# A two-layer decoder step on one Trainium2 core: RMS norms by sums with tokens on partitions, own buffers for raw mixer weights, other orders at the start of gate/up and in the down rounds, wider feature rows

## The chip, the cores and the metric

The kernel runs on one core of a Trainium2 chip. Its engines are TensorE (PE in the profile, with weight loads as PEld), VectorE (DVE), ScalarE (ACT), GpSimd (POOL) and SyncE (SP), which issues most DMAs; POOL issues others. The metric is the device time of one execution in microseconds (us). Before the change it is 2952.68 us, the median of 3 runs (2951.64 to 2955.0).

## The reference

One inference step of a two-layer decoder: an mLSTM layer (layer 0), then a forgetting-attention layer (layer 1). There are 1104 token rows (16 meta tokens, 1024 prompt, 64 sample rows), D_MODEL is 1024, D_FF 2816. Each layer ends with the output projection of its mixer, added to the residual stream, and a SwiGLU block; between the layers a value/key projection of layer 1 reads the normed stream. Only the following is touched by the change:

```python
def rmsnorm(x, g):
    xf = x.astype(jnp.float32)
    r = lax.rsqrt(jnp.mean(xf * xf, axis=-1, keepdims=True) + EPS)
    return (xf * r * g.astype(jnp.float32)).astype(x.dtype)
...
    out = (h.reshape(B, T, HV).astype(xn.dtype) * jax.nn.sigmoid(og)) @ w_out
...
def swiglu(xn, w_gu, w_d):
    gu = xn @ w_gu
    return (jax.nn.silu(gu[..., :D_FF]) * gu[..., D_FF:]) @ w_d
```

Everything is computed to float32 accuracy: each operand of a product is split into a high and a low part (a cast, then a subtraction), and three matmuls (high x high, high x low, low x high) make one product.

## The kernel before

**Layout.** The stream H lies with features on partitions: 8 tiles of 128 features (KT = 8), 1104 tokens along a row, cut into four quarters t of 276 tokens (SL). `self.xs` holds the normed stream's high and low parts (xh, xl) as tiles of 128 x 8 x 1104; `self.X[t]` are its quarters.

**Norms.** While a quarter of H is finished, ACT squares each of its 8 tiles and POOL or DVE adds the squares up (`add_sq`, the add on L312) into a tile of 128 x 276 sums, one partial sum per partition. Then a matmul with a 128x128 tile of ones as stationary operand adds over the partitions and spreads the sum to all of them (L110 and L320, tile `nps`, 276 columns), ACT takes the root of 276 columns (L111, L322) and DVE makes the reciprocal in two halves of 138 columns (L115, L325). The result `nr` multiplies the 8 tiles; products are cast to xh and subtracted to xl. `norm_x` is a generator: its caller runs some steps of it after each unit of other work, so that the norm lies between matmuls in the order written out by hand. `TwoNorms` does the same for the second quarter of a pair and adds differences of the two quarters (steps `root`, `inverse`, `scaled`, `first` to `fifth`), which the gate/up and down products use: these are computed on 2x2 blocks with 7 products in place of 8 (Strassen's scheme in Winograd's form), block sums of weights being made on POOL (`sums`) and split like the weights (`split_sums`).

**Mixer weights and units (`mlp`, L399 on).** The eight column blocks of the output projection are loaded raw by SP (L438) into the two tiles `slots[0]`, `slots[1]` in turn and split (`split`, cast on ACT L243, subtraction on DVE L244). In layer 0 the first three come already split from a copy in memory (`woD`, L434). `unit(t, m, x)` multiplies block m with quarter t: 24 matmuls (L171 to L173) into one of 3 PSUM buffers (`po`, L424), an add into H on DVE (L451), square and sum. The quarters go 0, 1, 2, 3; in quarter 2 each unit is followed by one step of the first pair of norms, in quarter 3 by steps of quarter 2's norm and splits of the first gate/up weights. `TA`, the tiles for block differences, are allocated from the left pool `sp`; slots lie on the right of SBUF. The place to the left of the slots is used by the mixer's own tiles until it ends.

**Gate/up (`ffn`, L1255 on).** `Unit(x)` is one 128-column block of gate (x even) or up (x odd); its products m1 to m7 are 12 matmuls each (L1305) for two halves h of the tokens. A product opens or continues a PSUM bank; the `_out` functions copy (ACT L1334) or add (DVE L1286) banks into `fs` places; `done` applies Silu (L1315) or multiplies up with gate. From L1450 on, the first two units are interleaved by hand with the second pair's norm steps; after that a loop runs over the remaining units. PE, DVE and ACT have their orders fixed here.

**Down rounds.** Seven rounds multiply the hidden blocks with `w_down` (five rounds on both halves of the tokens, two on each half alone). A round sums over 11 hidden blocks in groups of two, the last one single: 6 iterations. At the head of each iteration stand the split of the weights and hidden rows of two iterations ahead (`w_split`, `h_split`) and the loads further ahead (`w_load` on SP, `h_load` on POOL, L1425, three `hr` loads ahead). Then for each of 4 row blocks come the matmuls (L1614), and in a round's last iteration the adds into H (L1286). `pend` collects squares and norms of finished quarters; `steps` are run two per iteration. In layer 0 the norm before the value rows (`after`, `first_values`) runs in these steps, in layer 1 the final norm (`final`, transposes L1665, output L1690).

Of the kernel before, what the change touches and what calls it, by code (L numbers as in the profile page):

```python
# [17 lines left out]
P = 128  # L18
# [14 lines left out]
SL = T // 4  # L33
TS = [(SL * i, SL * i + SL) for i in range(4)]
DONE = {0: (1, 0, 5), 1: (2, 3, 4), 3: (6, 7, 8)}
# [56 lines left out]
class TwoNorms:  # L92
# [14 lines left out]
    def root(self):  # L107
        net, nc = self.net, self.net.nc
        ps = self.pp.tile([P, 512], F32, name=net.uid("nps"), tag="n")
        nc.tensor.matmul(ps[:, :SL], net.ones, net.sums[self.s], start=True, stop=True)  # L110
# [17 lines left out]
    def second(self):  # L128
        net, nc, lo, hi, y1, y2 = self.net, self.net.nc, self.lo, self.hi, self.y1, self.y2
        self.t2 = [net.ny(net.uid("t2")) for z in range(2)]  # L130
        self.sub(y2[:, lo], y2[:, hi], y2[:, lo])
        nc.scalar.copy(self.x[0][:, lo], y2[:, lo])
        for z, t in enumerate(self.t2):
            self.sub(t, y2[:, 4 + 2 * z : 6 + 2 * z], y1[:, 2 * z : 2 * z + 2])
            nc.scalar.copy(self.T[2][0][:, 2 * z : 2 * z + 2], t)
# [3 lines left out]
        nc.scalar.copy(self.x[0][:, hi], y2[:, hi])  # L139
# [15 lines left out]
class Net:  # L155
# [138 lines left out]
    def place(self, nm):  # L294

        self.turn[nm] += 1
        a = (2 * (nm == "nq") + self.turn[nm] % 2) * SL
        return self.sq[:, a : a + SL]
# [15 lines left out]
    def norm_x(self, H, t, g, sp, pp, inplace=False, psum=False):  # L314
# [4 lines left out]
        ps = pp.tile([P, 512], F32, name=self.uid("nps"), tag="n")  # L319
        nc.tensor.matmul(ps[:, :n], self.ones, self.sums[t][:, :n], start=True, stop=True)  # L320
        r = self.nr
        nc.scalar.activation(r, ps[:, :n], AF.Sqrt, scale=1.0 / D, bias=self.eps)  # L322
        for a in range(0, SL, SL // 2):
            yield
            nc.vector.reciprocal(r[:, a : a + SL // 2], r[:, a : a + SL // 2])  # L325
# [39 lines left out]
    def run(self):  # L365
# [34 lines left out]
    def mlp(self, H, raws, w, l, heads=None, cb=None):  # L400
# [5 lines left out]
        with self.pool(self.uid("nsp")) as sp, self.pool(self.uid("npp"), bufs=2, space=PSUM) as pn:  # L406
# [14 lines left out]
            with ExitStack() as c:  # L421
# [7 lines left out]
                for m in range(KT):  # L429
# [15 lines left out]
                    if m % 2 and not heads:  # L445
                        load(nc.sync, m // 2)
# [2135 lines left out]
```

## Time and profile before

| | us |
|---|---|
| median of 3 runs | 2952.68 |
| profiled execution, whole | 2954.85 |
| its span | 2952.9 |
| mean granted clock of TensorE | 0.98 |
| layer 0: output projection, gate/up, down | about 435 to 1320 |
| value rows behind it | to about 1420 |
| layer 1: output projection, gate/up, down, end | about 2085 to 2953 |

Numbers of this one profiled execution are given in us from the span's start. A line number such as L1305 is that of the kernel before. "Busy" is time in which an engine has an instruction; PE's matmuls are pipelined, so the time that one takes in a stream (length of the stretch over their count) is shorter than the mean duration of one. The granted clock is a share of full speed: 1.00 in a stretch means that TensorE was not slowed there. Rows of waits give an engine and line, what it waited for, total us, how often, and the longest.

### The profile page before, as it was taken

What the parts mean: (1) busy time and instruction counts of PE and PEld (TensorE: products, weight loads), DVE (VectorE), ACT (ScalarE), POOL (GpSimd) and SP (SyncE); (2) the same over time, 40 slices, a digit from 0 to 9 for tenths busy, and PEclk for the clock granted to TensorE, in tenths of its full rate; (3) what the DMA queues carried; (4) which work ended last, traced back from release to release, by engine and by line L of the source; (5) the groups of instructions that cost most, each with busy time, mean ns of one, the idle gap of its engine ahead of it and who ended that gap; (6) DMA issues with size and microseconds to landing.
All of it is one profiled execution on the core that took longest, in us unless ns stands there. A gap on an engine that the chain in (4) does not pass through costs nothing.

```text
span 2952.9 us, 60240 instructions
## 1 busy us (share of the span) xinstructions
PE 2807.9 (95%) x23457; PEld 2684.7 (91%) x23457; DVE 1797.3 (61%) x3908; ACT 1173.1 (40%) x2292; POOL 854.9 (29%) x1304
## 2 busy tenths in 40 slices
PE   7999988889999999989999899999898999999998
PEld 7999878889999999989999887677888999999998
DVE  4132555868888665593355443677476888866555
ACT  5222462322323233453344453777333232323344
POOL 2011333322323322235352201454232232323111
PEclk9999998999999999999999999999999999999998
DMA  6353546235555375664443675352423555537555
GB/s 193 104 136 100 135 126 195 72 95 176 161 177 160 112 230 173 207 200 135 148 164 128 223 281 211 122 169 85 146 75 94 177 159 177 162 98 237 191 172 188
DMA packets 428279, 464.70 MB, mean 157 GB/s; under 512 B 42434, under 2 KB 353338, under 8 KB 426970
## 3 DMA queue, kind: packets, MB, share of 16 engines
q1 hardware_dynamic: 382722, 317.83, 34.9%
q0 software_dynamic: 42864, 141.57, 14.8%
q8 instruction: 184, 3.01, 0.4%
q10 hardware_dynamic: 2408, 1.46, 0.2%
q14 instruction: 101, 0.83, 0.1%
HBM read 318.77 MB, written 141.96 MB: 156 GB/s over the span
## 4 chain that ended last, share of the span: by engine, by line
PE 75%; DVE 8%; ACT 3%; issue 3%; DMA 2%; POOL 0%; SPq 0%; DVEq 0%; ACTq 0%; POOLq 0%
PE m L1305 31%; PE dps L1614 14%; PE tmps L172 3%; PE tmps L171 3%; PE tmps L173 3%; PE sp L2377 2%; PE op L2464 1%; PE pops L173 1%; PE pops L172 1%; DVE s L2381 1%; PE pops L171 1%; PE mmA L171 1%; DVE slot L244 1%; PE bps L171 1%; PE tp L2431 1%
## 5 line engine op out<-in xcount | busy, mean ns | idle before, releaser
L1305 PE MATMUL m<-xh,slot 128*128 128x276 f32 x2752 | 542.4, 291 | 7.8 <-ACT fs L1334 3.7
L1305 PEld LDWEIGHTS m<-xh,slot 128*128 128x128 f32 x2752 | 440.8, 189 | 9.8 <-issue 4.5
L1305 PE MATMUL m<-xl,slot 128*128 128x276 f32 x1376 | 398.0, 289 | 0.2
L1305 PEld LDWEIGHTS m<-xl,slot 128*128 128x128 f32 x1376 | 259.6, 189 | 0.6 <-DVE xl L102 0.6
L244 DVE TENSOR_TENSOR slot<-slot,slot 128x1024 fp32r<-128x1024 f32 x138 | 181.2, 1314 | 115.7 <-ACT slot L243 113.9
L171 PE MATMUL tmps<-slot,xh 128*128 128x256 f32 (+2 forms) x864 | 244.5, 283 | 0.0
L172 PE MATMUL tmps<-slot,xh 128*128 128x256 f32 (+2 forms) x864 | 243.2, 281 | 0.0
L173 PE MATMUL tmps<-slot,xl 128*128 128x256 f32 (+2 forms) x864 | 243.1, 281 | 0.0
L243 ACT CAST slot<-slot 128x1024 fp32r<-128x1024 f32 x138 | 144.1, 1045 | 201.4 <-PE m L1305 109.9
L173 PEld LDWEIGHTS tmps<-slot,xl 128*128 128x128 f32 (+1 forms) x864 | 159.0, 184 | 0.0
L171 PEld LDWEIGHTS tmps<-slot,xh 128*128 128x128 f32 (+1 forms) x864 | 158.6, 184 | 0.1
L172 PEld LDWEIGHTS tmps<-slot,xh 128*128 128x128 f32 (+1 forms) x864 | 158.5, 183 | 0.1
L171 PE MATMUL mmA<-xh,whi 128*128 128x384 f32 (+1 forms) x384 | 134.6, 350 | 0.0
L172 PE MATMUL mmA<-xl,whi 128*128 128x384 f32 (+1 forms) x384 | 127.6, 332 | 0.0
L173 PE MATMUL mmA<-xh,wlo 128*128 128x384 f32 (+1 forms) x384 | 127.3, 332 | 0.0
L244 DVE TENSOR_TENSOR slot<-vA,slot 128x1024 fp32r<-128x1024 f32 x59 | 82.8, 1403 | 35.4 <-ACT slot L243 32.4
L244 DVE TENSOR_TENSOR slot<-Ht,slot 128x1024 fp32r<-128x1024 f32 x59 | 82.5, 1399 | 35.7 <-ACT slot L243 32.7
L243 ACT CAST slot<-Ht 128x1024 fp32r<-128x1024 f32 x59 | 61.5, 1043 | 105.5 <-PE m L1305 99.6
L243 ACT CAST slot<-vA 128x1024 fp32r<-128x1024 f32 x59 | 61.4, 1042 | 105.7 <-PE m L1305 97.8
L2404 ACT ACTIVATE s<-s,nb 128x272 f32<-128x272 f32 (+7 forms) x126 | 98.9, 787 | 0.0
L1403 DVE TENSOR_TENSOR ws<-ws 128x128 f32<-128x128 f32 x264 | 91.8, 348 | 9.0
L2439 ACT COPY th<-tp 128x768 f32<-128x768 f32 (+1 forms) x80 | 73.5, 919 | 56.8 <-PE tp L2431 33.2
(738 smaller groups left out, 8713.9 us busy)
## 6 DMA issues: line engine op xcount, KB each, us to landing
slot<-sD SPq DMA_DIRECT2D x48, 512.0 KB, 4.2
ws<-in_w_down SPq DMA_DIRECT2D x176, 128.0 KB, 2.7
sD<-ws SPq DMA_DIRECT2D x176, 128.0 KB, 2.2
slot<-in_w_gate_up SPq DMA_DIRECT2D x36, 512.0 KB, 3.8
kp<-in_cache_k SPq DMA_DIRECT2D x32, 512.0 KB, 5.8
vp<-in_cache_v SPq DMA_DIRECT2D x32, 512.0 KB, 5.8
vA<-in_w_gate_up SPq DMA_DIRECT2D x26, 512.0 KB, 3.8
Ht<-in_w_gate_up SPq DMA_DIRECT2D x26, 512.0 KB, 4.1
```

What stands on the lines that cost most here:

```text
L171: mm(ps, sh, mh, start=first, stop=False)
L172: mm(ps, sh, ml, start=False, stop=False)
L173: mm(ps, sl, mh, start=False, stop=last)
L243: self.nc.scalar.copy(hi, src)
L244: self.nc.vector.tensor_tensor(out=lo, in0=src, in1=hi.bitcast(F32), op=ALU.subtract)
L1305: nc.tensor.matmul(u.ps[h, b], w[p][:, k], x[q][:, k], start=first and k == i == 0, stop=k == 3 and i == 2, skip_group_check=True)
L1403: tt(out=o, in0=a, in1=b, op=ALU.subtract)
L1614: nc.tensor.matmul(o, p[:, k, ms], q[:, k], start=fresh and k == x == 0, stop=last and k == nk - 1 and x == 2, skip_group_check=True)
L2377: nc.tensor.matmul(ps[z][:, :n], a[r, qs], b[r, at : at + n], start=(y == 0), stop=(y == 2))
L2381: nc.vector.tensor_tensor_reduce(out=ss[z, u][:, at + o : at + e], in0=ps[z][:, o:e], in1=diag[x][:, z] if y else ncb[:, z, at + o : at + ...
L2404: nc.scalar.activation(ss[z, u], ss[z, u], AF.Exp, bias=nb[:, z : z + 1], accum_out=sm[:, u, z : z + 1])
L2439: nc.scalar.copy(th.rearrange("p x z (u h q) -> p h (x z u) q", h=2, q=64)[:, :, :n], pt[:, :, :n])
```

## The change

- **Norms.** The sum over partitions turns round: three matmuls take 92 columns of the sums as stationary operand and one column of ones as moving operand, so that 92 x 3 tokens lie on partitions (`Net.root`). The root and the reciprocal are taken of 92 x 3 numbers; DVE multiplies the identity with them to 92 x 276, a matmul with ones spreads the result over all partitions, and ACT copies it to `nr` (`Net.inverse`).
- **`norm_x`** yields after the root and after the inverse, and can wait some steps before the first (two in `after` for t < 3).
- **Raw buffers.** The raw mixer weights get six buffers of their own on the right of SBUF, next to the slots; they are closed after the loop and `TA` is allocated in their place. The PSUM pool `po` has 4 buffers.
- **Orders in `mlp`.** In quarter 2 the steps of the pair of norms start one unit later; in quarter 3 the steps of the norm are 0, 1, 1, 2, 1, 1, 1, 0 per unit.
- **Start of gate/up.** The split of the second unit's weights and the next load stand behind g.m1; `second` is cut into three steps; splits of sums and weights move ahead of products; u.m6 moves behind m4, which takes two more adds per half.
- **Down rounds.** The single group is the third of six; in a round's last iteration the splits and loads ahead come behind its adds; in layer 1 one step per iteration is run.
- **Wider rows.** The x tiles are allocated with 48 unused columns ahead of the 1104. The descriptor space of POOL's DMAs (`dynamic_dma_scratch_size`) is 4096 in place of 8192.
- **Value rows.** The steps of the last norm are spread 0, 2, 2, 2, 1, rest.

```diff
     def root(self):
-        net, nc = self.net, self.net.nc
-        ps = self.pp.tile([P, 512], F32, name=net.uid("nps"), tag="n")
-        nc.tensor.matmul(ps[:, :SL], net.ones, net.sums[self.s], start=True, stop=True)
-        nc.scalar.activation(self.r, ps[:, :SL], AF.Sqrt, scale=1.0 / D, bias=net.eps)
+        self.f = self.net.root(self.s, self.pp)
     def inverse(self):
-        for a in range(0, SL, SL // 2):
-            self.net.nc.vector.reciprocal(self.r[:, a : a + SL // 2], self.r[:, a : a + SL // 2])
+        self.net.inverse(self.f, self.pp)
...
+    def root(self, t, pp):
+        nc = self.nc
+        ps = pp.tile([P, 512], F32, name=self.uid("nps"), tag="n")
+        for c in range(3):
+            nc.tensor.matmul(ps[:NR, c : c + 1], self.sums[t][:, NR * c : NR * c + NR], self.ones[:, :1], start=True, stop=True)
+        f = self.place("nf")[:NR]
+        nc.scalar.activation(f[:, :3], ps[:NR, :3], AF.Sqrt, scale=1.0 / D, bias=self.eps[:NR])
+        return f
+
+    def inverse(self, f, pp):
+        nc = self.nc
+        nc.vector.reciprocal(f[:, :3], f[:, :3])
+        d = self.place("nq")[:NR].rearrange("p (c n) -> p c n", c=3)
+        nc.vector.tensor_tensor(out=d, in0=self.ident[:NR, :NR].unsqueeze(1).broadcast_to([NR, 3, NR]),
+                                in1=f[:, :3].unsqueeze(2).broadcast_to([NR, 3, NR]), op=ALU.mult)
+        ps = pp.tile([P, 512], F32, name=self.uid("nps"), tag="n")
+        nc.tensor.matmul(ps[:, :SL], self.ones[:NR], d.rearrange("p c n -> p (c n)"), start=True, stop=True)
+        nc.scalar.copy(self.nr, ps[:, :SL])
...
-            self.xs = [xp.tile([P, KT, T], F32R, name=f"x{s}") for s in "hl"]
+            self.xs = [xp.tile([P, KT, PX + T], F32R, name=f"x{s}")[:, :, PX:] for s in "hl"]
...
-            TA = self.turned(sp, f"{l}A")
...
-                pp = c.enter_context(self.pool(self.uid("po"), bufs=3, space=PSUM))
+                pp = c.enter_context(self.pool(self.uid("po"), bufs=4, space=PSUM))
+                raws_open = ExitStack()
+                rp = raws_open.enter_context(self.pool(self.uid("woraw"), side="right"))
...
-                    raw = cut(slots[m % 2 if cb else 1 - m % 2])
+                    raw = rp.tile([P, KT, P], F32, name=self.uid("woraw"), tag="woraw", bufs=6)
...
+                raws_open.close()
+                TA = self.turned(turned.enter_context(self.pool(self.uid("TA"), side="right")), f"{l}A")
...
-                    (n.root, n.inverse, n.scaled, n.first, n.second, n.third, n.fourth, n.fifth)[m]()
+                    for step in ((), (n.root,), (n.inverse,), (n.scaled, n.first), (n.second,), (n.third,), (n.fourth,),
+                                 (n.fifth,))[m]:
+                        step()
...
-                    for _ in range((3, 1, 1, 1, 1, 0, 0, 0)[x]):
+                    for _ in range((0, 1, 1, 2, 1, 1, 1, 0)[x]):
...
             def m6_out(u, h):
+                if u.late:
+                    for t, i, o in ((2, 1, u.v[h]), (1, 1, u.o[h])):
+                        add(o, o, u.ps[h, 2])
+                        u.done(h, t, i, o, o)
                 add(u.c[h], u.c[h], u.ps[h, 2])
...
-        groups = [(j, j + 1) for j in range(0, NC - 1, 2)] + [(NC - 1,)]
+        groups = [(0, 1), (2, 3), (4,), (5, 6), (7, 8), (9, 10)]
...
-        weights.split(1, 0, a1)
-        weights.load(2)
         g, u = Unit(0), Unit(1, [a1, weights.parts(1)[0][1]])
...
         g.m1(0)
         n.root()
         g.m1_out(0)
+        weights.split(1, 0, a1)
+        weights.load(2)
         g.m6(0)
         n.inverse()
-        g.m2(0)
         g.m6_out(0)
-        g.m2_out(0)
+        go(g, 0, "m2")
         n.scaled()
...
+        weights.split_sums(1, 1)
+        go(g, 1, "m4")
         weights.split(1, 1)
-        weights.split_sums(1, 1)
-        g.m3(1)
-        g.m3_out(1)
+        go(g, 1, "m3")
         weights.split_sums(1, 0)
...
-        u.do("m6")
         weights.split(2, 0)
         u.do("m7", "m5")
         weights.split_sums(2, 1)
         u.do("m4")
         weights.split(2, 1)
-        u.do("m3")
+        u.do("m6", "m3")
...
-                w_split(i + 2)
-                while at < len(items) and items[at][0] == i + 2:
-                    h_split(at)
-                    at += 1
-                w_load(i + 5)
+                def ahead(i=i):
...
+                if not last:
+                    ahead()
...
+                if last:
+                    ahead()
...
-                for _ in range(2):
+                for _ in range(2 if after else 1):
                     next(steps, None)
...
-        for _ in range(2 if i < 5 else 99):
+        for _ in range((0, 2, 2, 2, 1, 99)[min(i, 5)]):
...
-    nc = _bacc.Bacc("TRN2", target_bir_lowering=False, num_devices=1, dynamic_dma_scratch_size=8192)
+    nc = _bacc.Bacc("TRN2", target_bir_lowering=False, num_devices=1, dynamic_dma_scratch_size=4096)
```

More of the change, by code (lines that the diff above doesn't have):

```diff
@@ L33 @@
 SL = T // 4
+NR = SL // 3
 TS = [(SL * i, SL * i + SL) for i in range(4)]
+PX = P - T0
 DONE = {0: (1, 0, 5), 1: (2, 3, 4), 3: (6, 7, 8)}
@@ L138, in second @@
             self.low(self.T[2][1][:, 2 * z : 2 * z + 2], t, self.T[2][0][:, 2 * z : 2 * z + 2])
-        nc.scalar.copy(self.x[0][:, hi], y2[:, hi])
+        self.net.nc.scalar.copy(self.x[0][:, hi], y2[:, hi])
+    def second(self):
+        self.second_a()
+        self.second_b()
+        self.second_c()
     def third(self):
@@ L318, in norm_x @@
         n = t1 - t0
-        ps = pp.tile([P, 512], F32, name=self.uid("nps"), tag="n")
-        nc.tensor.matmul(ps[:, :n], self.ones, self.sums[t][:, :n], start=True, stop=True)
+        for _ in range(wait):
+            yield
+        f = self.root(t, pp)
+        yield
+        self.inverse(f, pp)
         r = self.nr
[L322 to L325, printed above, removed]
+        yield
         xh, xl = self.X[t]
@@ L526, in mlp @@
                 self.slots = slots
-            with cw if not cb else ExitStack():
+            with cw if not cb else ExitStack(), turned:
                 each = lambda t, m, x: self.add_sq(H, t, m, sp, x, KT - 1 if t < 3 else KT - 4)
@@ L1296, in __init__ @@
                 u.a = a or b
-                u.ps, u.c, u.v = {}, {}, {}
+                u.ps, u.c, u.v, u.o, u.late = {}, {}, {}, {}, a is not None
             def product(u, h, b, w, x, first):
@@ L1359, in m5_out @@
                 add(u.v[h], u.v[h], u.ps[h, 4])
-                u.done(h, 2, 1, u.v[h], u.v[h])
+                if not u.late:
+                    u.done(h, 2, 1, u.v[h], u.v[h])
             def m4(u, h):
@@ L1365, in m4_out @@
             def m4_out(u, h):
-                o = place()
+                o = u.o[h] = place()
                 add(o, u.c[h], u.ps[h, 3])
-                u.done(h, 1, 1, o, o)
+                if not u.late:
+                    u.done(h, 1, 1, o, o)
             def m3(u, h):
```

74 lines of the change are left out of this document (40 added, 34 removed).

## The prediction

> **What bounds the kernel now.** I read first the head of the page, with the busy time of each engine.
>
> ```profile
> span 2952.9 us, 60240 instructions
> ...
> PE 2807.9 (95%) x23457; PEld 2684.7 (91%) x23457; DVE 1797.3 (61%) x3908; ACT 1173.1 (40%) x2292; POOL 854.9 (29%) x1304
> ```
>
> TensorE is busy for all but 145 us, and the change takes no matmul of the products away. What can be gained is time in which PE stands still or runs at a lower clock, so I next read windows around the code that the change touches. Columns: stretch, its length, busy time (instructions) of PE, weight loads, DVE, ACT, POOL, then granted clock, DMA share, GB/s.
>
> ```profile
> 467.00:481.00 14.00, 5.79 (x26) 5.56 (x27) 7.35 (x10) 3.78 (x6) 4.11 (x6) 0.65 0.71 209
> ...
> 517.50:574.50 57.00, 48.41 (x369) 46.92 (x367) 45.48 (x65) 19.95 (x33) 22.35 (x23) 1.00 0.22 72
> 574.50:622.00 47.50, 37.23 (x246) 35.51 (x247) 31.55 (x52) 17.26 (x27) 10.19 (x10) 0.89 0.26 76
> 622.00:1230.00 608.00, 607.91 (x4770) 606.91 (x4769) 440.37 (x778) 194.93 (x305) 171.22 (x164) 1.00 0.54 166
> 1230.00:1314.00 84.00, 72.82 (x535) 71.52 (x534) 77.19 (x125) 50.65 (x99) 27.84 (x38) 0.96 0.69 223
> 2084.00:2103.00 19.00, 12.50 (x83) 11.68 (x80) 6.62 (x9) 3.57 (x5) 4.39 (x3) 0.82 0.78 220
> ...
> 2171.00:2201.00 30.00, 24.69 (x176) 23.75 (x174) 21.33 (x28) 9.04 (x17) 14.20 (x17) 0.94 0.44 132
> 2201.00:2246.00 45.00, 36.45 (x240) 34.49 (x241) 31.30 (x50) 17.22 (x27) 9.97 (x10) 0.89 0.27 81
> 2868.00:2940.00 72.00, 64.20 (x473) 62.84 (x472) 45.64 (x74) 36.64 (x67) 8.06 (x15) 0.93 0.62 197
> ```
>
> The fourth row is the yardstick: 608.00 us for 4770 matmuls without a stop, 0.1275 us each. A stretch's matmuls times 0.1275, taken from its length, leave its excess: 10.7 us (467), 10.0 (517.5), 16.1 (574.5), 15.8 (1230), 8.4 (2084), 7.6 (2171), 14.4 (2201), 11.7 (2868), together 94.7 us. All the rest of the long gate/up and down loops has none. I call the stretches A (mixer weights; 467 and 2084), B (second half of the output projection; 517.5 and 2171), C (start of gate/up; 574.5 and 2201) and D (end of the down rounds; 1230 and 2868); 1 and 2 are the layers. The waits of PE say who makes the excess (columns: total us, times, longest). A1, then A2:
>
> ```profile
> PE pops L172 <- DVE xl L244: 8.4, 2, 8.2
> ...
> PE pops L171 <- ACT slot L243: 4.3, 1, 4.3
> PE pops L173 <- DVE slot L244: 2.2, 2, 1.8
> ```
>
> B1, then B2 (whose first row is already the first product of C):
>
> ```profile
> PE pops L171 <- DVE vA L451: 3.8, 3, 1.4
> PE nps L110 <- DVE sq L312: 2.1, 1, 2.1
> PE nps L320 <- DVE sq L312: 0.8, 1, 0.8
> ...
> PE m L1305 <- DVE Ht L451: 2.1, 1, 2.1
> PE nps L320 <- DVE sq L312: 2.0, 1, 2.0
> PE pops L171 <- DVE Ht L451: 1.2, 1, 1.2
> ```
>
> C1; then D1; then D2:
>
> ```profile
> PE m L1305 <- ACT slot L243: 4.2, 1, 4.2
> PE m L1305 <- DVE vA L451: 2.1, 1, 2.1
> PE m L1305 <- ACT fs L1334: 1.8, 1, 1.8
> PE m L1305 <- DVE fs L1286: 1.6, 1, 1.6
> PE m L1305 <- DVE slot L244: 1.1, 1, 1.1
> PE nps L110 <- DVE sq L312: 0.7, 1, 0.7
> ...
> PE dps L1614 <- DVE vA L1286: 9.5, 3, 4.0
> ...
> PE dps L1614 <- DVE Ht L1286: 5.3, 2, 3.8
> PE fin L1665 <- DVE Ht L1690: 2.4, 2, 1.9
> ```
>
> **The norms' new price.** There are 12 such norms, 8 in layer 1 and 4 in layer 2. Each loses one sum on PE, a Sqrt over 276 columns and two reciprocals on DVE; it gains three small matmuls (two passes each, being float32), a small Sqrt, a small reciprocal, a DVE multiply of 276 columns, a broadcast matmul of the old sum's size and an ACT copy.
>
> ```profile
> L325 DVE RECIPROCAL vA<-vA 128x138 f32<-128x138 f32 x6 | 6.0, 1008 | 2.2 <-ACT vA L322 2.2
> L341 DVE TENSOR_TENSOR xl<-npy,xh 128x276 fp32r<-128x276 f32 x24 | 10.5, 438 | 0.3
> L1687 DVE RECIPROCAL fr<-fr 128x1 f32<-128x1 f32 x8 | 1.3, 164 | 4.0 <-ACT fr L1686 4.0
> L2214 PE MATMUL mps<-ktS,qmt 128*128 128x16 f32 x16 | 2.0, 259 | 0.0
> ```
>
> DVE: 2 x 1.01 goes, 0.16 + 0.44 comes, 1.4 us less per norm. PE: a matmul of a few columns costs 2.0/16 = 0.125 us of PE's time (row L2214), 0.259 if none overlaps the next, so six cost 0.75 to 1.55; I take 0.8, since they stand back to back, and the broadcast replaces the old sum at the same cost. New too is a round trip PE to ACT to DVE to PE: the work in it is about 0.25 (a small Sqrt, estimated at half of a 276-column pass, 0.44) + 0.16 + 0.44 = 0.85 us; three hand-overs at 0.4 us, the step of "issue" in the chain of waits quoted under A, make it 2.0. Bounds are 0.85 (hand-overs free) and 3.3 (twice as dear). Where another unit of 24 matmuls (3.06 us) lies between root and inverse, only what DVE still has queued shows; I take 0.9 there, from 0 to 2.0. The small weights come in as six loads.
>
> The Trainium skill, page "TensorE: Matmul & The Clock Gate", section "LDWEIGHTS (loading the stationary operand)", says that a weight load takes time by the columns it loads, not by what it is used for. That speaks against this change, which makes the sums stationary: 92 columns are paid six times to move one column. By its figure the six loads would be an estimated 0.46 us, and the sum below about 4 us lower over 12 norms; the row L2214 (0.125 us for 16 columns moved) decides for the dearer price.
>
> **A, six raw buffers.** Before, the raw weights share two slots, so a load waits for the split two before it. First SP's row (start, length, five issues), then pieces of the chain of waits (start, length, what):
>
> ```profile
> 445.42 23.22 SPq L438 DMA_DIRECT2D slot<-in_w_out_a  x5
> ...
> 460.12 0.43 issue
> ...
> 462.26 10.00 DMA slot<-in_w_out_a
> ```
>
> Five issues stretch over 23.22 us, and the transfer that the chain enters at 462.26 lands at 472.3; PE has run out by then. With six buffers SP issues all at once; the transfers' sum does not shrink (DMA share 0.71 in the stretch), and behind them on SP stands the first gate/up load, which now also goes out earlier. In A1 10.7 us are excess: 8.4 wait, 2.3 clock. I let 4.7 stay for the last raw and its splits (0.1275 x 24 = 3.06 us for one unit that waits, and 1.6 clock), so -6. The first norm runs root and inverse back to back there: +0.8 +2.0. A1: **-3.2**. In A2 the waits are 6.5 and the clock 1.9; the six buffers can be loaded while attention still runs, if their place is free. 8.4 - 0.8 (root) leaves 7.6; I take **-5**, as the earlier steps may keep a unit's wait (2.2 of the rows above). If the place is still attention's, the raws come later than the two that were loaded early: 0 to +2.
>
> **B, norm steps one unit later, a fourth PSUM buffer.** The root at m=1 rather than 0 has unit (2,1), 3.06 us, over its 2.1 wait; the second norm's root moves to x=1 over its 0.8 (2.0 in layer 2). The fourth buffer gives each add 3.06 us more, over 3.8 and 1.2 (longest 1.4). The first bank of C was held by the last adds (2.1); with four buffers the first bank's last user is two units earlier. B1 with that bank: -2.1 -0.8 -3.8 -2.1 +2 x (0.8 + 0.9) = **-5.4**; B2: -2.0 -1.2 -2.1 +3.4 = **-1.9**. If DVE (45.48 of 57.00 us busy) uses up the cover, the 3.8 returns.
>
> **C, another order at the start of gate/up.** The split of the second half's weights now stands after the first product, so its ACT cast (wait 4.2) and DVE part (1.1) no longer stand ahead of what PE needs first; the other splits are spread between products, and the late m6 of the odd unit adds two DVE adds per half (4 x 0.44 us), under PE's 16 products there. Rows of C1 without the bank: 4.2+1.8+1.6+1.1+0.7 = 9.4, and 16.1 - 11.5 = 4.6 clock or small waits. What comes: root 0.8; the broadcast has only one product of 12 matmuls (1.53 us) over it and a DVE pass in front, I take the full 2.0; the sums' 0.7 stays; one half-clock spell of 3.4 us in place of the spells now, 1.7. C1: -14.0 + 5.2 = **-8.8**. C2, whose excess is 1.7 less: **-7.1**.
>
> **D, single group in the middle, adds before splits, fewer steps.**
>
> ```profile
> 1126.64 8.54 DVE L1286 TENSOR_TENSOR vA<-vA,dps 128x276 f32<-128x276 f32 x24 [3.01 <-PE dps L1614]
> ```
>
> In D1 DVE is busy 77.19 of 84.00 us: moving adds ahead does not help while DVE has the same work, only its 3 x 1.4 less does: **-4** (0 to -8). In D2 DVE has room (45.64 of 72): the wait of 5.3 for the adds goes when a round's last splits stand behind them, and 2.4 as the final steps come one per iteration; with the clock that is 11.7, of which I take **-7**. In two-half rounds the largest batch of adds (24 in 8.54 us) now stands ahead of two splits which have two iterations of 48 matmuls (12.2 us) to finish: 8.54 and the splits of three tiles come close to that; I take half a microsecond a layer, **+1**. The norm in the value rows behind D1 waits for its sums as those in B do; its new root and its cover cost about as much: zero.
>
> **Wider rows and less descriptor space.** Matmuls that read rows of different pitch cost the same already:
>
> ```profile
> L1305 PE MATMUL m<-xh,slot 128*128 128x276 f32 x2752 | 542.4, 291 | 7.8 <-ACT fs L1334 3.7
> ...
> L1614 PE MATMUL dps<-T0A_2h,slot 128*128 128x276 f32 x64 | 12.8, 292 | 1.8 <-DVE vA L1286 1.8
> ```
>
> I take zero; 1 ns over the 2752 of this row, half as many with the low part and as many again in the projections bounds it at ±8 us. Half the descriptor space: zero, see the third rival.
>
> **Sum.** -3.2 -5 -5.4 -1.9 -8.8 -7.1 -4 -7 +1 = -41.4. The profiled run took 2954.85 us, 1.95 more than its span, and 2.17 more than the median of the runs (2952.68): 2954.85 - 41.4 = 2913.4 for such a run, **2911** for the median.
>
> **Rivals.** First, waits only move: DVE ends last in B and C after the reorder, since it keeps nearly all its work there (45.48 of 57, 31.55 of 47.5). Half the gain, -21: 2932. Against it: DVE loses 1.4 per norm and the named waits are of order, not of load.
>
> Second, the round trip stops PE at all 12 norms and lowers its clock after: 12 x (2.0 + 1.7) = 44 in place of the 13 counted above (2.0 + 4 x 0.9 + 2 x 2.0 + 2 x 1.7), so -41.4 + 31 = -10: 2942. For it: the 2171 stretch has a clock of 0.94 with no wait longer than 2.1. Against: a unit of 3.06 us lies between the steps in most places. The Trainium skill, the same page, section "What's actually happening", has the clock fall only after an idle window of some 3.4 us; by that rule these stops would cost 2.0 alone, and this case would end near 2922. The row of 2171 does not bear the rule out for stops this short.
>
> Third, slower: the halved descriptor space lets POOL hold only one load of hidden rows in flight.
>
> ```profile
> hr<-hB_0T POOLq DMA_DIRECT2D x20, 276.0 KB, 3.8
> ```
>
> An iteration of a two-half round takes 48 x 0.1275 = 6.1 us and needs two: 2 x 3.8 - 6.1 = 1.5, 30 iterations in each of 2 layers, 90; a one-half iteration takes 3.06 and needs one: 0.74 x 24 x 2 = 36. With the gain: 2911 + 126 = 3037. It decides as soon as fewer than two such loads fit; with two nothing changes. Against it: with the three loads that the kernel keeps ahead, a landing of 3.8 us shows none standing in line for space at twice the size.
>
> Fourth, A2's buffers come late: +7 on the sum, 2918. Fifth, the wider rows cost or save 8.
>
> **How the numbers follow.** Forecast 0.55 (2900 to 2922 by its own bounds), first rival 0.2, second 0.1, third 0.07, the rest 0.08. The low end takes the round trips of A1 and C at 0.85 (-3.5), no clock spell in C (-3.4), 4 more from D1, 4 more in A (the 4.7 gone), and 8 saved by the rows: 2911 - 23 = 2888. The high end takes in the first two rivals: 2943. Faster by over 0.2% (5.9 us, about what a measurement of this kernel tells from no change): 0.85; same 0.05 (the second rival with costlier rows); slower 0.10 (the third, and the second with all bounds against it).
>
> **What would show it.** Right: the 8.4 wait for L244 in A1 and the 4.2 for L243 in C are gone, PE idles under 10 us from 574 to 620, reciprocals of 138 columns have given way to ones of 3, and the gate/up and down loops keep 0.1275 us per matmul. Wrong: new waits of PE for the multiply at the broadcast over 2 us in most norms; waits of PE for hr splits all through the down rounds; a changed matmul spacing in 622 to 1230.

## The result, and the profile after

The changed kernel takes 2949.31 us (median of 20 runs, 2942.42 to 2961.68), the kernel before 2953.27 in 20 runs beside them. The ratio is 0.9988 with a 95% interval of 0.9976 to 1.0000: some 4 us faster, next to nothing, where 41 had been forecast. The profiled execution of the changed kernel (span 2957.5 us, 2959.58 in all) is one of its longer ones, so stages are compared, not ends. A stage here runs from the first matmul of one kind to that of the next (the down rounds and the value rows to the last of their own), in us, each from one profiled execution:

| stage | before | changed | old norm (e1) | late broadcast (e3) |
|---|---|---|---|---|
| units, layer 0 (A1, B1) | 129.4 | 127.1 | 111.7 | 122.8 |
| gate/up, layer 0 (C1) | 487.2 | 485.6 | 489.4 | 482.3 |
| down, layer 0 (D1) | 253.0 | 265.9 | 255.1 | 250.5 |
| value rows and what follows | 327.8 | 323.1 | 321.8 | 327.9 |
| to the first unit of layer 1 | 441.7 | 450.3 | 447.3 | 442.1 |
| units, layer 1 (A2, B2) | 116.7 | 116.4 | 105.7 | 112.1 |
| gate/up, layer 1 (C2) | 484.8 | 485.8 | 490.8 | 482.7 |
| down, layer 1 (D2) | 254.3 | 241.9 | 242.8 | 242.8 |

D2 won 12.4 us and D1 with the value rows lost 8.2 (about 5 and 11 in the profiles of e5 and e6 below, whose down rounds are the same); A, B and C, on which most of the forecast rested, stand where they stood. Most of the waits that were to go have gone: none of the rows quoted of before for L1305 behind casts (4.2), for adds of units (3.8) or for the split in A1 (8.4) has a counterpart; only A2's wait for the cast of the first split is still there (4.3 before, 5.8 now). PE's waits in the changed kernel have other names. In columns as before, first B1 with the start of C1 (520 to 590), then the same of layer 1 with A2 (2090 to 2240), then the end of D1 with the norm of the value rows (1240 to 1345):

```profile
PE nps L341 <- DVE sq L338: 10.2, 3, 8.4
PE nps L328 <- DVE sq L321: 7.6, 2, 7.1
...
PE nps L341 <- DVE sq L338: 8.8, 3, 7.0
PE nps L328 <- DVE sq L321: 8.7, 2, 7.1
PE pops L180 <- ACT slot L252: 5.8, 1, 5.8
...
PE nps L341 <- DVE sq L338: 11.1, 4, 5.7
PE dps L1656 <- DVE T0A_4l L253: 4.3, 2, 2.2
PE dps L1656 <- DVE T0B_2l L253: 1.7, 1, 1.7
PE dps L1656 <- DVE T0A_1l L253: 0.9, 2, 0.5
```

L328 is the root's matmul, waiting for the last square sum (L321); L341 is the broadcast, waiting for DVE's multiply of the identity (L338). The broadcast alone holds PE for 30 us in these stretches. Five of the twelve broadcasts wait more than 2 us (8.4, 7.0, 5.7, 2.2 and 2.1). PE is slower behind such stops too: from 558.6 to 562.2, behind the one of 8.4, the granted clock is 0.50, and matmuls follow each other every 0.23 us in place of 0.127; behind a stop of 2.2 it is 0.50 from 1275.8 to 1279.0. Over 520 to 575 the clock (the third number from the end) was 1.00 before and is now 0.91:

```profile
520.00:575.00 55.00, 48.17 (x366) 46.94 (x367) 43.05 (x60) 19.29 (x32) 22.29 (x22) 1.00 0.23 75
520.00:575.00 55.00, 44.81 (x333) 43.87 (x332) 35.52 (x47) 16.05 (x26) 19.70 (x21) 0.91 0.23 73
```

What DVE does while PE waits 8.4 us is seen in its timeline (start, length, operation; in brackets idle time before):

```profile
544.46 1.21 DVE L321 TENSOR_TENSOR sq<-sq 128x276 f32<-128x276 f32 x1 [0.63 <-ACT sq L319]
545.59 4.32 DVE L104 TENSOR_TENSOR xl<-vA,xh 128x1104 fp32r<-128x1104 f32 x1
549.84 0.43 DVE L485 TENSOR_TENSOR vA<-vA,pops 128x276 f32<-128x276 f32 x1
551.70 1.84 DVE L253 TENSOR_TENSOR slot<-slot,slot 128x1024 fp32r<-128x1024 f32 x1 [1.43 <-ACT slot L252]
553.46 0.43 DVE L485 TENSOR_TENSOR vA<-vA,pops 128x276 f32<-128x276 f32 x1
555.38 1.41 DVE L253 TENSOR_TENSOR slot<-slot,slot 128x1024 fp32r<-128x1024 f32 x1 [1.49 <-ACT slot L252]
556.72 0.43 DVE L485 TENSOR_TENSOR vA<-vA,pops 128x276 f32<-128x276 f32 x1
557.07 0.16 DVE L336 RECIPROCAL sq<-sq 92x3 f32<-92x3 f32 x1
557.33 0.44 DVE L338 TENSOR_TENSOR sq<-ident,sq 92x276 f32<-92x276 f32 x1
```

The reciprocal and the multiply take 0.6 us. They stand behind a 4.32 us pass, three adds and two splits; each split waits for its cast on ACT. Before, PE ran on through this backlog; now the broadcast stands in PE's own order, and PE has to wait until DVE has caught up. In D1 the broadcast follows the root with no other matmul between them, and ACT is a link too:

```profile
1244.11 0.57 PE L328 MATMUL nps<-ones,sq 128*92 128x1 f32 x6
1250.38 1.26 PE L341 MATMUL nps<-sq,ones 92*128 92x276 f32 x2 [5.69 <-DVE sq L338]
...
1246.38 1.04 ACT L252 CAST slot<-slot 128x1024 fp32r<-128x1024 f32 x1 [2.22 <-DMA slot<-sD]
1247.34 0.65 ACT L252 CAST T0B_1h<-hr 128x552 fp32r<-128x552 f32 x1
1248.00 1.28 ACT L330 ACT_TABLE_LOAD   x1
1249.29 0.26 ACT L330 ACTIVATE sq<-nps,eps 92x3 f32<-92x3 f32 x1
```

The root's matmuls start at 1244.11; the Sqrt of 276 numbers stands behind a cast that waits for a weight transfer, and behind a table load of 1.28. The broadcast follows at 1250.38, a stop of 5.7 us for a chain whose own work (0.26, 0.17 and 0.44 us) is under 1.

### The profile page after: what moved, and what is told of

Read it like the earlier page. It is cut to its first block, busy times and chain, and to the rows that moved or that the text cites. A ratio compares the mean times of both kernels' runs of the same rounds, so it can differ in the third digit from the quotient of the medians.

```text
span 2957.5 us, 60404 instructions
## 1 busy us (share of the span) xinstructions
PE 2798.9 (95%) x23529; PEld 2678.4 (91%) x23529; DVE 1790.7 (61%) x3916; ACT 1173.4 (40%) x2304; POOL 850.6 (29%) x1304
## 4 chain that ended last, share of the span: by engine, by line
PE 74%; DVE 8%; ACT 3%; issue 3%; DMA 2%; POOL 1%; DVEq 0%; SPq 0%; POOLq 0%; ACTq 0%
PE m L1341 31%; PE dps L1656 14%; PE tmps L180 3%; PE tmps L182 3%; PE tmps L181 3%; PE sp L2421 1%; PE op L2508 1%; PE pops L182 1%; PE pops L180 1%; PE pops L181 1%; DVE s L2425 1%; DVE slot L253 1%; PE mmA L180 1%; PE bps L180 1%; PE tp L2475 1%
## 5 line engine op out<-in xcount | busy, mean ns | idle before, releaser
L253 DVE TENSOR_TENSOR slot<-slot,slot 128x1024 fp32r<-128x1024 f32 x130 | 172.2, 1324 | 60.1 <-ACT slot L252 58.8
L252 ACT CAST slot<-slot 128x1024 fp32r<-128x1024 f32 x130 | 135.9, 1045 | 137.1 <-PE m L1341 111.8
L180 PE MATMUL mmA<-xh,whi 128*128 128x384 f32 (+1 forms) x384 | 134.2, 349 | 0.1
L253 DVE TENSOR_TENSOR slot<-vA,slot 128x1024 fp32r<-128x1024 f32 (+1 forms) x59 | 81.5, 1384 | 35.8 <-ACT slot L252 34.7
L253 DVE TENSOR_TENSOR slot<-Ht,slot 128x1024 fp32r<-128x1024 f32 (+1 forms) x59 | 81.3, 1380 | 35.8 <-ACT slot L252 34.7
L252 ACT CAST slot<-Ht 128x1024 fp32r<-128x1024 f32 (+1 forms) x59 | 61.0, 1036 | 97.7 <-PE m L1341 93.8
L252 ACT CAST slot<-vA 128x1024 fp32r<-128x1024 f32 (+1 forms) x59 | 60.9, 1035 | 97.8 <-PE m L1341 95.8
```

What stands on the lines that cost most here:

```text
L180: mm(ps, sh, mh, start=first, stop=False)
L252: self.nc.scalar.copy(hi, src)
L253: self.nc.vector.tensor_tensor(out=lo, in0=src, in1=hi.bitcast(F32), op=ALU.subtract)
```

## The experiments

Each ran 4 to 12 times beside the kernel before; "ratio" is against before, with its 95% interval. The changed kernel stands at 0.9988 (0.9976 to 1.0000). A difference from it, or between two experiments, is that of the ratios times 2953 us. Line numbers shift from kernel to kernel: `nps <- DVE sq` stands for the broadcast's wait with L338 (L341 in e3 and the runs made from it, L326 in e2), and for the root's wait for the last square sum with L321 (L324 in e3 and the runs made from it).

**e1, the old norm in the changed kernel.**

```diff
     def root(self, t, pp):
-        for c in range(3):
-            nc.tensor.matmul(ps[:NR, c : c + 1], self.sums[t][:, NR * c : NR * c + NR], self.ones[:, :1], start=True, stop=True)
...
+        nc.tensor.matmul(ps[:, :SL], self.ones, self.sums[t][:, :SL], start=True, stop=True)
+        nc.scalar.activation(self.nr, ps[:, :SL], AF.Sqrt, scale=1.0 / D, bias=self.eps)
     def inverse(self, f, pp):
-        nc.vector.reciprocal(f[:, :3], f[:, :3])
...
+        for a in range(0, SL, SL // 2):
+            nc.vector.reciprocal(self.nr[:, a : a + SL // 2], self.nr[:, a : a + SL // 2])
```

> The changed kernel with the old norm in its place: one sum matmul that spreads to all partitions, root of 276 columns, two reciprocals of 138; all orders, buffers, pitch and groups stay as changed. Theory A (the new norm's broadcast matmul stands in PE's order behind everything that ACT and DVE still have queued, and these stops, 32 us in the changed kernel's profile, give back what the orders gained): 18 to 28 us faster than the changed kernel, about 2925; no wait of PE over 3 us between 545 and 560 or at the norms of the down rounds; 7 us waits for the sums ahead of the root at 577 and 2218 stay. Theory B (DVE ends last in these stretches whatever the norm): within 6 us of the changed kernel, with the same stops at adds in place of the broadcast.

Measured: 2931.97 us, ratio 0.9927 (0.9911 to 0.9942), 18 us less than the changed kernel. The stop at the broadcast is gone, but the wait for the sums ahead of the second pair's root has not stayed at 7. From 520 to 600:

```profile
PE nps L327 <- DVE sq L321: 12.6, 2, 12.1
PE m L1333 <- DVE fs L1314: 1.5, 1, 1.5
```

So the norm costs what theory A says, and theory B holds for part: without the broadcast PE reaches the next point at which it needs DVE sooner and waits there.

**e2, the new norm alone in the kernel before** (the counterpart of e1's diff).

> The kernel before with the new norm alone; orders, buffers, pitch, groups as before. Theory A: 12 to 25 us slower than before (2965 to 2978), with waits of PE at the broadcast of 2 us and more in most of the 12 norms. Theory B: within 6 us of before; PE's stops at the broadcast replace stops that were there.

Measured: 2967.96 us, ratio 1.0052 (1.0037 to 1.0068), 15 us slower than before. From 500 to 600 its longest wait is of the same kind:

```profile
PE nps L329 <- DVE sq L326: 11.2, 4, 7.8
```

Only two of its twelve broadcasts wait more than 2 us (7.8 and 6.6, both in quarter 3), where most were expected to; those of its down rounds wait 1.1 to 1.8. With e1 this gives the norm's price from both sides: 15 us put into the old orders, 18 taken out of the new ones.

**e3, the broadcast one step later.**

```diff
                                 in1=f[:, :3].unsqueeze(2).broadcast_to([NR, 3, NR]), op=ALU.mult)
+        return d
+
+    def spread(self, d, pp):
+
+        nc = self.nc
         ps = pp.tile([P, 512], F32, name=self.uid("nps"), tag="n")
...
-        self.inverse(f, pp)
+        d = self.inverse(f, pp)
+        yield
+        if wait:
+            yield
+        self.spread(d, pp)
...
-                    for step in ((), (n.root,), (n.inverse,), (n.scaled, n.first), (n.second,), (n.third,), (n.fourth,),
+                    for step in ((), (n.root,), (n.inverse,), (n.spread, n.scaled, n.first), (n.second,), (n.third,), (n.fourth,),
...
-                    for _ in range((0, 1, 1, 2, 1, 1, 1, 0)[x]):
+                    for _ in range((0, 1, 1, 3, 1, 1, 1, 0)[x]):
...
-                        return self.norm_x(H, t, None, sp, pn, psum=t < 3, wait=2 * (t < 3))
+                        return self.norm_x(H, t, None, sp, pn, psum=t < 3, wait=t < 3)
...
         go(g, 0, "m2")
+        n.spread()
         n.scaled()
```

(The first norm takes its steps as 1, 1, 5 from unit (1, 5) on. With `wait=t < 3` the root of the norms in the down rounds also moves, one iteration ahead.)

> The changed kernel with the broadcast matmul and its copy one step later than the reciprocal and the multiply (one unit in the mixer, one product at the start of gate/up, one iteration in the down rounds). Theory A, if the stops are latency that a unit of 3 us covers: 8 to 15 us faster than the changed kernel, the stops of 5.9, 2.4 and 2.3 in the down rounds gone and the 8.6 down by 3. Theory A, if they are backlog of DVE: the 8.6 and 7.2 stay within 2 us, 3 to 8 us faster by the down rounds alone. Theory B: no gain (within 4 us).

Measured: 2924.08 us, ratio 0.9901 (0.9883 to 0.9918), 26 us less than the changed kernel and more than forecast; it is no slower than the old norm. Waits of PE from 520 to 590, then the broadcast's row from 1225 to 1345:

```profile
PE nps L349 <- DVE sq L341: 5.4, 1, 5.4
PE nps L331 <- DVE sq L324: 4.7, 2, 3.9
PE m L1353 <- DVE fs L1334: 1.3, 1, 1.3
...
PE nps L349 <- DVE sq L341: 1.3, 1, 1.3
```

In D1 the stops were latency: iterations between the root, the multiply and the broadcast cover them, 11.1 us of waits become 1.3, and the stage falls from 265.9 to 250.5. The value rows behind it are 4.8 us longer, so 10.6 of the 15.4 are kept. Whether the earlier root or the later broadcast counts more there was not tried apart. In quarter 3, where only the broadcast moved, the stop is backlog: 8.4 falls by the 3 us of one unit, to 5.4.

**e4, the down rounds of the first layer as before** (groups and splits at the head of an iteration where `after` is given; the second layer as changed).

> The changed kernel with groups and the place of the splits in the down rounds of the first layer as before; second layer as changed. In the changed kernel that stretch lost 13 us against before, the second layer's won 12. Theory A (the norms make this loss): 0 to 5 us better than the changed kernel, since its stops at the broadcast (5.9, 2.4, 2.3) stay and the 6.6 us of waits for split hidden rows (2.4, 2.0, 2.3) are paid for by the 9.5 us of waits for adds that return. Theory C (the single group in the middle and the late splits make it): 6 to 12 us faster than the changed kernel.

Measured: 2940.71 us, ratio 0.9960 (0.9946 to 0.9974), 8 us less than the changed kernel: theory C by the number. Waits for adds return (5.2 us, three times), waits for the broadcast halve (5.9 us, four times).

**e7, the same with the late broadcast of e3.**

> The broadcast one step later (as in e3) and the down rounds of the first layer as before (as in e4). If the two add up: 2924 - 8 = 2916. If the late splits cost only because the stops at the broadcast made everything late: no gain on e3, 2921 to 2928, as the waits for the adds of a round (9.5 us before) return.

Measured: 2932.10 us, ratio 0.9921 (0.9908 to 0.9934): no gain on e3; the intervals meet. So the order in D1 is not dear by itself: without the immediate broadcast the stage takes 249.3 in the old order and 250.5 in the new, with it 253.3 (e4) and 265.9. That the broadcast then waits for the splits that now come late is the likely reason; no run shows it apart.

**e5, the raw weights in two slots again.**

```diff
-                    raw = rp.tile([P, KT, P], F32, name=self.uid("woraw"), tag="woraw", bufs=6)
+                    raw = cut(slots[m % 2 if cb else 1 - m % 2])
```

> The changed kernel with the raw mixer weights in the two slots in turn, as before; all else as changed. If six buffers gain what was forecast for them (11 us in A1 and A2): 8 to 13 us slower than the changed kernel. If the early loads only move the wait, since in A1 the first split weights from memory then land later (PE waits 11.4 us for them in the changed kernel against 6.9 before) and in A2 the raws wait for the attention's place (6.0 us at the first product against 6.5 over two waits before): within 4 us of the changed kernel, the 11.4 back near 7 and the 8.4 for the split back.

Measured: 2961.04 us, ratio 1.0016 (1.0004 to 1.0029), 8 us slower than the changed kernel, at the edge of the first expectation. In the profiles the units of both layers are 7.1 and 8.0 us shorter with six buffers (127.1 and 116.4 against 134.2 and 124.3), but the first unit of layer 0 starts 6.0 us later. Waits of PE around 430 to 480, changed kernel, then e5:

```profile
PE pops L180 <- DMA wo<-woD: 11.4, 1, 11.4
```

```profile
PE pops L180 <- DMA wo<-woD: 8.2, 1, 8.2
PE pops L181 <- DVE xl L253: 7.5, 1, 7.5
```

SP's rows of the changed kernel say why (start, length, issue):

```profile
433.97 2.56 SPq L470 DMA_DIRECT2D woraw<-in_w_out_a  x2
436.92 8.48 SPq L466 DMA_DIRECT2D wo<-woD  x6
445.50 10.40 SPq L470 DMA_DIRECT2D woraw<-in_w_out_a  x3
```

Two raw loads, free to go, are issued ahead of the split weights that the first unit needs. In layer 1 the first unit waits 5.8 us for its raw (quoted above), where two slots make it 3.0 and 2.2.

**e6, x rows of 1104 and descriptor space of 8192 again.**

> The changed kernel with x rows of 1104 again and the descriptor space at 8192 again. If both are worth nothing, as the matmul spacing of the gate/up loops (0.127 us in both profiles) has it: within 4 us of the changed kernel. If the wider rows gain or the smaller space costs: more than 5 us off, in the spacing of the gate/up loops or in waits for hidden rows.

Measured: 2955.39 us, ratio 0.9997 (0.9988 to 1.0005); the interval overlaps that of the changed kernel. The two were taken back together, so effects against each other would not show. From 625 to 1060 PE has 3413 matmuls in 433.42 busy us and the changed kernel 3422 in 434.82: 0.127 us each.

**e8, old norm in the units, late broadcast elsewhere** (e3 with e1's norm where `inplace` is set and in the first pair).

> e3 with the old norm in the three norms of each mixer's units (DVE there does 1.4 us more per norm, PE never waits for the broadcast), the late broadcast kept at the start of gate/up and in the down rounds. If the stretch of the units is held by the synchronisation of PE with DVE's backlog: 5 to 12 us faster than e3 (2912 to 2919), the 5.5 us stop there gone. If by DVE's load: within 4 us of e3, the stop moved to the sums at the start of gate/up (12.3 us with the old norm everywhere).

Measured: 2929.39 us, ratio 0.9913 (0.9898 to 0.9927): within 5 us of e3. The units take 113.9 in place of 122.8 us, gate/up behind them 490.5 in place of 482.3, with the stop at the sums:

```profile
PE nps L331 <- DVE sq L324: 12.1, 1, 12.1
```

**e12, e1 with the start of gate/up in its old order.**

> e1 (all as changed but for the old norm) with the start of gate/up in its old order. If the reorder there is worth what was forecast (about 6 to 9 us a layer, without the new norm's own costs): 12 to 18 us slower than e1 (2944 to 2950). If PE stands at this place for DVE's backlog whatever the order (12.3 us wait for the sums of quarter 3 in e1): within 5 us of e1 (2932).

Measured: 2941.17 us, ratio 0.9944 (0.9927 to 0.9962), between the two expectations: 5 us by the ratios, 9 by the medians. The two intervals overlap, so the whole times do not settle it. The gate/up stages of the profiles are 6.0 and 6.4 us longer than e1's. From 555 to 640 the waits of before stand there again, behind the wait for the sums:

```profile
PE nps L327 <- DVE sq L321: 12.1, 1, 12.1
PE m L1333 <- ACT slot L252: 4.2, 1, 4.2
PE m L1333 <- ACT fs L1362: 1.7, 1, 1.7
PE m L1333 <- DVE slot L253: 1.1, 1, 1.1
```

The reorder does take away what it was meant to (none of these three casts and copies has a row of its own in e1); the 12.1 in front of it is untouched by it.

**e9, splits of the first gate/up weights from units 0 and 1 of quarter 3 to units 3 and 4.**

```diff
-                    if x < 2:
-                        weights.split(0, x)
-                    elif x == 2:
-                        weights.load(1)
+                    if 3 <= x < 5:
+                        weights.split(0, x - 3)
+                    elif x == 5:
+                        weights.load(1)
...
+                    if 5 <= x < 7:
+                        weights.split_sums(0, x - 5)
```

> e3 with the two splits of the first gate/up weights moved from units 0 and 1 of quarter 3 to units 3 and 4 (the splits of sums to 5 and 6, the next load and sums behind them), so that only adds and squares stand between the fifth step of the first pair and the reciprocal. If the stop of 5.5 us at the broadcast in quarter 3 comes from these two casts and subtractions (3.3 us of DVE, ACT waiting for DVE and the other way round): stop under 2.5 us and 3 to 6 us faster than e3 (2924). If DVE's load sets the end: the stop shrinks, and the wait for the sums behind g.m1 (4.0) or for weights grows by as much; within 3 us of e3.

Measured: 2923.89 us, ratio 0.9891 (0.9877 to 0.9906), as e3. From 520 to 590 the stop moved with nearly its whole length, from the broadcast to the sums:

```profile
PE nps L331 <- DVE sq L324: 8.2, 2, 7.4
PE nps L349 <- DVE sq L341: 1.4, 2, 1.3
```

What DVE does per unit is plain in its timeline; PE's unit is 3.06 us, and in a unit with a split DVE takes 566.51 - 561.82 = 4.7 from one split to the next. Of these it idles 1.2 (0.78 + 0.42), so its work alone, 3.5, is more than PE's unit:

```profile
561.82 1.23 DVE L256 TENSOR_TENSOR slot<-slot,slot 128x1024 fp32r<-128x1024 f32 x1 [1.65 <-ACT slot L255]
562.96 0.73 DVE L405 TENSOR_TENSOR xl<-vA,xh 128x552 fp32r<-128x552 f32 x1
563.60 0.91 DVE L392 SCALAR_TENSOR_TENSOR vA<-vA,gain 128x276 f32<-128x276 f32 x2
564.44 0.43 DVE L497 TENSOR_TENSOR vA<-vA,pops 128x276 f32<-128x276 f32 x1
565.64 0.45 DVE L324 TENSOR_TENSOR sq<-sq 128x276 f32<-128x276 f32 x1 [0.78 <-ACT sq L322]
566.51 1.22 DVE L256 TENSOR_TENSOR slot<-vA,slot 128x1024 fp32r<-128x1024 f32 x1 [0.42 <-ACT slot L255]
```

**e10 and e11, POOL's block sums ahead of quarter 2 (alone, and with e9).** In both the sums are written over part of quarter 0 of H while the first pair's differences still read it, so that the products of gate/up and all that follows work with other numbers; instructions and sizes are the same.

```diff
                 run = norm(2)
-                weights.sums(0)
...
+                weights.sums(0)
                 for m in range(KT):
                     unit(2, m, m)
```

> e3 with POOL's four block sums of the first gate/up weights ahead of quarter 2 rather than ahead of quarter 3. In e3 DVE's pass that makes the low part of quarter 1 takes 4.3 us while POOL computes these sums, the same pass elsewhere 1.3 to 1.9. If POOL's sums slow it: the pass takes under 2.2 us, the stop at the broadcast falls by about 2, and the kernel is 1 to 4 us faster than e3, some slower passes in quarter 2 allowed. If the pass is slow for another reason: 4.3 stays, within 2 us of e3.

> e9 and e10 together. If both act on DVE's backlog: 5 to 9 us faster than e3 (2915 to 2919); if only load counts: within 3 us of e9.

Measured: 2917.34 us, ratio 0.9872 (0.9858 to 0.9886), and 2919.95, 0.9881 (0.9864 to 0.9898). In e10 the pass of 4.32 us takes 1.30; PE waits 6.7 us at the sums. By the ratios e10 is 9 us faster than e3, more than expected, with intervals that just meet, and e11 3 us faster than e9, with intervals that overlap. Since both compute something else, only the length of the pass is taken from them.

**e13, the same sums behind unit 3 of quarter 3**, where their place is free (e9 with `if x == 3: weights.sums(0)`).

> e9 with POOL's block sums of the first gate/up weights behind unit 3 of quarter 3 rather than ahead of quarter 3. If POOL's sums slow DVE's pass of 4.3 us beside them: that pass takes 1.3 to 2, PE's wait for the sums of quarter 3 ahead of the second pair's root falls from 7.6 to 4 to 6 us in each layer, and the kernel is 3 to 7 us faster than e9. If the contention only moves to the passes beside the sums' new place: the pass is short, other passes grow by as much, the wait stays within 1 us of 7.6 and the time within 3 us of e9.

Measured: 2924.41 us, ratio 0.9899 (0.9880 to 0.9917). DVE's timeline:

```profile
547.18 1.29 DVE L104 TENSOR_TENSOR xl<-vA,xh 128x1104 fp32r<-128x1104 f32 x1
...
551.76 2.18 DVE L341 TENSOR_TENSOR sq<-ident,sq 92x276 f32<-92x276 f32 x1
```

The pass is short and the multiply, now beside the sums, takes 2.18 in place of 0.44; PE's wait at the sums is 8.6 (7.0 in layer 1) against e9's 7.4 (7.5). The second expectation holds: the slowdown goes where POOL's sums go.

**e14, two of DVE's last square sums of quarter 3 on POOL** (late=KT - 1 for all quarters).

> e9 with two of the three last square sums of quarter 3 that DVE makes given to POOL. If DVE's load alone sets the wait of 7.6 us: it falls by 1 to 2 us. If what sets it is the chain add on DVE, square on ACT, sum, each in line behind splits: it stays or grows, since a sum on POOL takes 0.8 to 1.3 us against 0.45 on DVE. Either way within 4 us of e9.

Measured: 2921.87 us, ratio 0.9897 (0.9882 to 0.9912); the wait stays at 7.4. Two sums of 0.45 us are not what sets it. Which part of DVE's work and of its waits for ACT does is not shown.

## Why the prediction was wrong

**The norm's price: the total near, the places wrong.** The terms held 12 us for it, net (eight roots of 0.8 and 9.6 of stops, less 4 of D1); e1 and e2 show 15 to 18. That the totals are near is luck. The six small matmuls take 0.57 to 0.65 us rather than 0.8 in ten of the norms, and 1.08 behind the two waits of 7.1; the Trainium skill's page "TensorE: Matmul & The Clock Gate", section "LDWEIGHTS (loading the stationary operand)", led to an estimate of 0.46, so the ten lie between. What was wrong is the stop: the sum charged 9.6 us for it, and the profiled execution of the changed kernel stops for 31.3 us at its twelve broadcasts. The step said "Where another unit of 24 matmuls (3.06 us) lies between root and inverse, only what DVE still has queued shows; I take 0.9 there, from 0 to 2.0". What DVE and ACT had queued held PE for up to 8.4 us. The upper bound of 2.0 was the chain's own length, which bounds nothing where the chain stands in line behind other work; where hardly anything is queued, at the first norm (root and inverse back to back), the stop is 1.2. And the three norms in D1 had no price at all in the sum, neither root nor stop, though root and broadcast stand back to back there.

**B and C: the step that failed.** -5.4, -1.9, -8.8 and -7.1 were forecast, 23 us with the norms' own costs in them. The stages of A, B and C together moved by -3.9 in layer 0 and +0.7 in layer 1, and the six buffers' gain in A (7.1 and 8.0 of these stages by e5) is in this. Each wait was taken off as if PE then ran on. The rows named DVE and ACT, but the excess was held by DVE's pace: 4.7 us per unit with a split in quarter 3 against PE's 3.06 (e9). Taking the waits away one by one sends PE to the next place at which it needs DVE: the broadcast (8.4), or the sums ahead of the pair's root (12.1 with the old norm, 7.4 in e9), as e1, e8, e9 and e12 show. The prediction wrote "If DVE (45.48 of 57.00 us busy) uses up the cover, the 3.8 returns", and its first rival, at 0.2, said as much; it returned as 8.4 and 7.1 in layer 0. The busy share (45.48 of 57.00 us) had looked like room, but DVE's idle time there is waits for ACT's casts, which wait for DVE in turn.

**C's reorder** is worth some 6 us a layer by the profiles of e12 and e1 (5 to 9 for both layers by the whole times, not clear of noise). Forecast were 8.8 and 7.1 with 2.8 for the new norm's root and broadcast in each, so 11.6 and 9.9 for the order itself: the mechanism was right, the size about twice too large, and the stop before it grew meanwhile.

**A: right in kind, a little smaller.** -3.2 and -5 were forecast, which without the norm's own costs is about 6 each for the buffers; e5 shows 8 us for both. Two details differ: the first split weights land 3 us later (8.2 to 11.4), as two raws pass them on SP, and in layer 1 the first raw is waited for (5.8, and 6.5 in two waits before), which the fourth rival had named. So the wait that A2 was to save is still there; the 8.0 us by which e5's units of layer 1 are longer lie behind it and are not traced.

**D1: wrong in sign.** -4 was forecast from "DVE is busy 77.19 of 84.00 us", +8.2 came with the value rows. The stops at the broadcast (11.1 us) and late splits (6.9) outweigh the adds' 9.5, and e3, which moves only steps of the norm, takes 10.6 us of it back, value rows included. So it was not DVE's load, which e3 leaves as it is, that set this stage in the changed kernel, but where the norm's steps stand in PE's order. **D2: right, larger.** -7 was forecast, -12.4 came, and it came in every kernel with this order: 5.3 + 2.4 us of waits went, and the stage's clock is 1.00 in place of 0.98. Which of its three parts (groups, splits, steps) makes it was not tried.

**Rows and descriptor space**: nothing that can be told from zero, as forecast (e6).

**The rivals.** The first (2932, waits only move) and the second (2942, stops at the norms) were worked out as alternatives; both happened in part and at once (of the second the stops in five norms, with the lower clock behind each of them), and 2949 lies beyond each, 6 us above the range. The third did not: hidden rows land in 3.6 to 4.7 us in the changed kernel, against 3.8 to 4.6.

## What to carry to other kernels

Before a wait is counted as a gain, compare what the engine it names does per unit of work with the bound engine's unit; if that engine is slower there, the wait will reappear at the next dependence, whatever its name. A step that sends PE's result through ACT and DVE back to PE costs what stands in those queues, not its own length (here up to 8.4 us for a chain of under 1); put a unit of independent matmuls between the last step off PE and the matmul that needs it. Here that move of a few steps (e3, or e9 with it: 2924 us) turned a change worth 4 us into one worth 29.

## What the hardware showed

A DVE pass with two operands in SBUF, 128 x 1104, takes 4.32 us where POOL computes two block sums of 1.36 us during it, and 1.29 us without (e9 and e13), and the multiply of 92 x 276 goes from 0.44 to 2.18 when the sums are moved beside it. The Trainium skill, page "SBUF — State Buffer", section "Who interferes with whom", says that a DVE instruction with two SBUF inputs contends with a GpSimd instruction that reads SBUF; the traces agree.

An execution's stage to the first unit of layer 1 varied from 435.3 to 450.3 us between kernels whose code is the same there, apart from the raw loads at its end; a single profile of this kernel cannot settle differences of 5 us by its end.
